# Where the sums of an attention are spread, how 16 leftover keys are multiplied, and how a final norm ends: three edits in one fused decoder kernel

## The chip, the core and the metric

The kernel runs on one core of a Trainium2 chip. The time is the device time of one execution in microseconds (us); lower is better. The engines are TensorE (PE in the profile, its weight loads PEld), VectorE (DVE), ScalarE (ACT), GpSimd (POOL) and SyncE (SP), which here issues nearly all transfers.

## What is computed

The reference is two layers of a decoder with two groups of heads. 16 learned "meta" tokens stand ahead of 512 tokens (T = 528), the model width D is 1024, all in float32. Per layer:

```python
xn = rmsnorm(h, attn_norm_g)
proj = xn @ w_in                      # q,k,v of 8 FoX heads (64 wide), a gate each; q,k,v,g of 4 retention heads (128 wide)
logf = log_sigmoid(flog + b_fgate)
# FoX: softmax(q.k / 8 + c[t] - c[s]) v over s <= t, with c = cumsum(logf)
# retention: sum over s <= t of gamma^(t-s) (q.k) v, then a group norm per head, times silu(g)
h = h + concat(fox, ret) @ w_out
hn = rmsnorm(h, ffn_norm_g)
h = h + (silu(hn @ w_gate) * (hn @ w_up)) @ w_down      # 2816 wide
```

Meta queries form a block of their own, real queries go in blocks of 128. After the second layer comes `rmsnorm(h, final_norm)`, and the first 16 tokens are dropped.

## The kernel before

**Layout and products.** Activations lie transposed: 128 features on the partitions, the 528 tokens along the free dimension. Each float32 operand is split into a high part that TensorE's fast float32 format holds exactly, and a low part (`split`, L136 to L138: ScalarE casts to `hi`, VectorE subtracts to get `lo`), so a product is two or three matmuls (`hi*hi`, `hi*lo`, `lo*hi`). Weights come from DRAM through SP into three `raw` buffers (L153); ScalarE casts them (L186), and GpSimd or VectorE subtract (L187). An output tile of a projection needs 24 matmuls of 264 columns twice (L210).

**Order.** TensorE's list is written out by hand: `layer` builds a `plan` in which the steps of attention and retention are merged at given places into the 128-wide projections (`merge`, `spread`, `ret_places`), and `manual_schedule` holds TensorE to it. The instructions of VectorE, ScalarE, GpSimd and SP are put in order by the scheduler, each engine works through its list in order, and `tc.high_priority()` moves what stands in it forward. PSUM has 8 banks: 4 in a ring `psa` (`psum_a()`) for scores, transposes and attention products, the rest for projections (`psd`). Scratch tiles of 128x528 in SBUF, called by tags as `tt("tq")`, `tt("ol")`, `tt("sq")`, `tt("sd")`, come from one ring "w" of four.

**FoX heads** go in four pairs per layer (`fox_steps`). `values` (transposes at L409) turns the pair's values into five blocks of keys: four of 128, and the last one of 16. `scores(s, b)` makes the scores of head s and query block b (L497), the bias and row minimum (L503, L504, L509) and the exponential on ScalarE with the row sums accumulated (L517). `turn` transposes the probabilities on TensorE (L409) and splits them into `pth` and `ptl`; the last 16 keys of four blocks are turned together by VectorE's 32x32 transpose (L521). `product(s)` multiplies values by probabilities, high and low: with 16 keys in the last block, too, there are two matmuls (L567); in layer 0 the meta queries have two of 16 columns (L559). Then `ol` and `mixt` (L570, L571) put the two halves together. The division by the row sums comes after the second head: at the last `scores` VectorE takes the reciprocal of `sums` (L525), ScalarE spreads it to a [128, 512] tile `tq` (L527), and in `product(1)` four transposes (L576) turn this into a PSUM bank, by which VectorE multiplies (L577). The result is split into `mxh`, `mxl` for the output projection.

**Retention heads** (`ret_steps`): `values` transposes (L409), subtracts the mean (L662, L663) and splits into `rvh`, `rvl`. `scores` multiplies q by k (L694), then VectorE by the decay (`sd`, L699), then a split into `rsh`, `rsl`; the last 16 keys go to small tiles `rs`. `product` (L724) has three matmuls per key block, so also for the last 16 keys.

**The end.** In the last layer the down-projection is in two column ranges, PA (272 columns) and PB (240). While the rows m = 0 to 7 of range b are made, `after_0` to `after_7` carry the norm of range a between them: squares, sums over rows by a matmul with ones (L1135), the reciprocal root as `Ln` and then `Exp` on ScalarE (L1122, L1123), one Newton step of three VectorE rows (L1127, L1129, L1131), and multiplications by the root (L1110), each followed by a store (L1113). GpSimd does out_a 0 and 2 and out_b 6; VectorE does the others. For range b everything after row 7 is behind the last matmul of the down-projection.

## Time and profile before

| | |
|---|---|
| runs | 1278.76, 1278.95, 1279.9 us; median 1278.95 |
| profiled execution | 1278.89 us, its span 1277.1 us |
| granted TensorE clock | 0.996 |
| instructions | 23190, of them 9265 matmuls |

The span is what the profile covers, from the first to the last instruction on the core; the execution's time is 1.8 us longer. Busy time is the time in which an engine had an instruction at work. Rows of the timeline give the start in us, the duration in us, the engine, the line, the operation, output and input, and the shape; where several rows of one kind follow closely they are joined, and xN says how many. In square brackets stands the idle time before a row, and what ended it.

### The profile page before, as it was taken

How to read it: one execution, taken by the hardware profiler on the slowest of the kernel's cores; microseconds unless marked ns; L12 is line 12 of the kernel's file. 1: busy time of each engine (PE TensorE's matmuls, PEld its weight loads, DVE VectorE, ACT ScalarE, POOL GpSimd, SP SyncE). 2: the span in 40 equal slices, each digit the busy share in tenths (PEclk: the TensorE clock that was granted, in tenths of full speed). 3: DMA queues.
4: the chain of work that ended last, by engine and by line, in shares of the span. 5: the costliest groups of instructions: out<-in, count | busy, mean ns of one | idle time of the engine just before them, and what ended most of it. 6: DMA issues, size and time to landing. Idle time of an engine off the chain costs nothing.

```text
span 1277.1 us, 23190 instructions
## 1 busy us (share of the span) xinstructions
PE 1258.0 (99%) x9265; PEld 1197.8 (94%) x9265; DVE 1019.4 (80%) x1849; ACT 687.7 (54%) x1250; POOL 181.0 (14%) x150
## 2 busy tenths in 40 slices
PE   9999999999999999999999999999999999999997
PEld 8899999999999999999999989999789999999996
DVE  7888866879988888887687878568899878888867
ACT  7566655576544444444455665456764444444445
POOL 2233333210000000000014334332000000000001
PEclk9999999999999999999999999999999999999998
DMA  6222222223323333332323122222223333333321
GB/s 233 76 67 84 75 84 84 66 73 115 107 97 100 100 100 100 100 100 83 100 76 112 65 100 84 77 91 66 100 83 130 102 100 100 100 100 100 103 79 67
DMA packets 45677, 120.55 MB, mean 94 GB/s; under 512 B 5360, under 2 KB 12272, under 8 KB 45568
## 3 DMA queue, kind: packets, MB, share of 16 engines
q1 hardware_dynamic: 45136, 118.77, 28.4%
q8 instruction: 73, 1.20, 0.4%
q10 hardware_dynamic: 432, 0.29, 0.1%
q14 instruction: 36, 0.29, 0.1%
HBM read 116.91 MB, written 2.13 MB: 93 GB/s over the span
## 4 chain that ended last, share of the span: by engine, by line
PE 84%; DVE 10%; ACT 4%; DMA 1%; issue 1%; DVEq 0%; POOL 0%; ACTq 0%
PE psd L210 24%; PE psa L875 18%; PE psd L1010 14%; PE psd L875 13%; PE psa L1010 4%; PE psa L210 3%; PE psa L409 2%; PE psa L497 1%; PE psa L567 1%; PE psa L724 1%; PE psa L694 1%; DVE qs L429 1%; DMA bc<-cdr 1%; DVE pr L504 1%; DVE rsl L138 0%
## 5 line engine op out<-in xcount | busy, mean ns | idle before, releaser
L187 POOL TENSOR_TENSOR wlo<-raw,whi 128x512 fp32r<-128x512 f32 x126 | 172.3, 1381 | 380.2 <-ACT whi L186 380.2
L210 PE MATMUL psd<-xh,whi 128*128 128x264 f32 (+1 forms) x792 | 195.8, 315 | 0.0
L210 PE MATMUL psd<-xl,whi 128*128 128x264 f32 (+1 forms) x792 | 186.5, 303 | 0.6 <-DVE xl L313 0.6
L210 PE MATMUL psd<-xh,wlo 128*128 128x264 f32 (+1 forms) x792 | 186.9, 303 | 0.0
L210 PEld LDWEIGHTS psd<-xh,whi 128*128 128x128 f32 x792 | 128.7, 190 | 4.7 <-ACT whi L186 0.4
L210 PEld LDWEIGHTS psd<-xh,wlo 128*128 128x128 f32 x792 | 127.2, 188 | 6.2 <-DVE wlo L187 0.4
L210 PEld LDWEIGHTS psd<-xl,whi 128*128 128x128 f32 x792 | 128.0, 189 | 5.2 <-DVE xl L313 1.2
L186 ACT CAST whi<-raw 128x512 fp32r<-128x512 f32 (+1 forms) x168 | 98.3, 613 | 39.2 <-PE psd L210 19.9
L863 ACT CAST whi<-raw 128x1024 fp32r<-128x1024 f32 (+2 forms) x62 | 54.9, 885 | 51.3 <-PE psd L875 39.9
L863 ACT CAST fwhi<-raw 128x1024 fp32r<-128x1024 f32 (+2 forms) x62 | 55.6, 897 | 48.1 <-PE psd L875 40.5
L864 DVE TENSOR_TENSOR wlo<-raw,whi 128x1024 fp32r<-128x1024 f32 (+2 forms) x62 | 62.9, 1014 | 13.7 <-ACT whi L863 13.6
L864 DVE TENSOR_TENSOR fwlo<-raw,fwhi 128x1024 fp32r<-128x1024 f32 (+2 forms) x62 | 64.0, 1032 | 10.8 <-ACT fwhi L863 10.5
L875 PE MATMUL psa<-th,whi 128*128 128x264 f32 (+1 forms) x232 | 65.4, 282 | 0.0
L875 PE MATMUL psa<-th,wlo 128*128 128x264 f32 (+1 forms) x232 | 65.4, 282 | 0.0
L875 PE MATMUL psa<-tl,whi 128*128 128x264 f32 (+1 forms) x232 | 65.3, 282 | 0.0
L875 PE MATMUL psa<-th,fwhi 128*128 128x264 f32 (+1 forms) x224 | 63.4, 283 | 0.0
L875 PE MATMUL psa<-tl,fwhi 128*128 128x264 f32 (+1 forms) x224 | 63.3, 283 | 0.0
L875 PE MATMUL psa<-th,fwlo 128*128 128x264 f32 (+1 forms) x224 | 63.3, 282 | 0.0
L517 ACT ACTIVATE pr<-pr,nmax 128x144 f32<-128x144 f32 (+1 forms) x64 | 36.9, 576 | 42.8 <-DVE nmax L504 30.5
L941 ACT COPY e<-psa 128x264 f32<-128x264 f32 (+1 forms) x114 | 42.9, 376 | 27.9 <-PE psa L875 23.6
L863 ACT CAST fwhi<-S 128x1024 fp32r<-128x1024 f32 x20 | 21.0, 1049 | 68.6 <-PE psa L875 66.5
L1010 PE MATMUL psd<-ah,fwlo 128*128 128x264 f32 (+1 forms) x200 | 56.6, 330 | 0.0
(355 smaller groups left out, 4008.6 us busy)
## 6 DMA issues: line engine op xcount, KB each, us to landing
raw<-w_in SPq DMA_DIRECT2D x54, 512.0 KB, 3.5
raw<-w_gate SPq DMA_DIRECT2D x44, 512.0 KB, 4.0
fraw<-w_up SPq DMA_DIRECT2D x38, 512.0 KB, 3.4
raw<-w_down SPq DMA_DIRECT2D x64, 256.0 KB, 2.7
raw<-w_out SPq DMA_DIRECT2D x16, 512.0 KB, 3.5
raw<-w_down SPq DMA_DIRECT2D x32, 192.0 KB, 2.5
bc<-cdr SPq DMA_DIRECT2D x16, 264.0 KB, 3.3
raw<-w_up SPq DMA_DIRECT2D x6, 512.0 KB, 3.5
```

The costliest lines, as they stand in the source:

```text
L186: pin(nc.scalar.copy(hi, job["raw"][:, c0:c1]), pinned)
L187: pin(sub(lo, job["raw"][:, c0:c1], hi.bitcast(F32)), pinned)
L210: nc.tensor.matmul(ps[1][b][:, 0:c1 - c0], w[:, wk, :], x[:, c0:c1], start=(k == 0 and i == 0), stop=(k == n - 1 and i == 2))
L409: nc.tensor.transpose(ps[:, 128 * j:128 * j + 128], src[:, o:o + 128], idt)
L429: nc.vector.tensor_sub(sv(t, real, b0, b1), sv(tq, real, a0, a1), sv(t, real, a0, a1).bitcast(F32))
L497: nc.tensor.matmul(sc[0:nq, 0:c1 - c0], st["q"][s][:, q0:q0 + nq], kk[:, c0:c1], start=(i == 0), stop=(i == 1))
L517: nc.scalar.activation(pr, pr, AF.Exp, bias=nmax[0:nq], scale=-1.0, accum_out=rsum)
L863: nc.scalar.copy(hi, src)
L864: nc.vector.tensor_sub(lo, src, hi.bitcast(F32))
L875: nc.tensor.matmul(bank()[:, 0:b.shape[-1]], a[:, o + k, :], b, start=(fresh and k == 0 and i == 0), stop=(k == n - 1 and i == 2), skip_gr ...
L941: nc.scalar.copy(self.t["e"][:, i], self.t["x"][:, 0:w])
L1010: nc.tensor.matmul(v[:, 0:c1 - c0], a[:, s * n + k, :], b[:, c0:c1], start=(k == 0 and i == 0), stop=(k == n - 1 and i == 2))
```

## The change

It has three parts.

**The sums' way (FoX).** The row sums of a pair lie in one of two persistent [128, 32] tiles. At the last `scores` step VectorE takes the reciprocals and turns the tile in 32x32 squares, both with priority. Four SP transfers write the turned rows to a DRAM tile [8, 128], two more read them back, each spread over 64 partitions, into a `tq` tile. `product(1)` multiplies `mixt` by this tile in SBUF. The four transposes, their PSUM bank and ScalarE's spread go.

**The last 16 keys, stacked.** The last block's 16 keys take 16 of 128 partitions. Now partitions 0 to 15 hold the high part, 32 to 47 the low part, and the values stand a second time on the same partitions (`repeat`, a ScalarE copy in `v_done`), so one matmul does both. The meta block of layer 0 lies at partitions 64 and 96 of the same tile with a third and fourth copy of values. In retention, high, low and again high parts (partitions 0, 32, 64) stand against the values' high part twice and low part once, so one matmul takes the place of three.

**The end.** All multiplications by the root are VectorE's, GpSimd has none. The reciprocal root is one ScalarE activation, `Abs_reciprocal_sqrt`, whose table set is loaded after the last silu in place of the one for logarithms. The steps `after_3` to `after_7` are put in another order: all three Newton rows of range a in `after_3`, its multiplications 0 and 2 in `after_3` and `after_4`; the low part of the sum of squares is made in `after_6`, and the last sums go in the order high, low, square 6, square 7 behind square 5.

```diff
+    sum_tiles = [state.tile([128, 32], F32, name=f"sums{i}") for i in range(2)]
+    for t in sum_tiles:
+        nc.gpsimd.memset(t, 0.0)
...
+    def repeat(vt, c0, n, at):
+        nc.scalar.copy(vt[:, at:at + 32 * n].rearrange("p (n c) -> p n c", c=32)[:, :, 0:META],
+                       vt[:, c0:c0 + META].unsqueeze(1).broadcast_to([128, n, META]))
...
@@ FoX v_done
+            repeat(vt, SEQ, 1, SEQ + 32)
+            if not real:
+                repeat(vt, 0, 2, SEQ + 64)
...
@@ FoX scores, last step
-                nc.vector.reciprocal(st["sums"], st["sums"])
-                st["rows"] = tt("tq")
-                nc.scalar.copy(st["rows"][:, 0:SEQ].rearrange("p (b s d) -> p b s d", b=NBLK, s=2),
-                               st["sums"].unsqueeze(3).broadcast_to([128, NBLK, 2, 64]))
+                sums = sum_tiles[g % 2]
+                turned = tmp.tile([128, 32], F32, name="turned", tag="turned")
+                with tc.high_priority():
+                    nc.vector.reciprocal(sums[:, 0:2 * NBLK], sums[:, 0:2 * NBLK])
+                    nc.vector.transpose(turned, sums)
+                rdr = tc.dram_tile([2 * NBLK, 128], F32, name=f"rdr{ly['l']}{g}")
+                for a in range(4):
+                    nc.sync.dma_start(rdr[:, 32 * a:32 * a + 32], turned[32 * a:32 * a + 2 * NBLK, :])
+                st["rows"] = tt("tq")[:, 0:SEQ]
+                wide = rdr.rearrange("(s b) q -> s (b q)", s=2)
+                for i, (a0, a1) in enumerate(ROWS):
+                    nc.sync.dma_start(st["rows"][a0:a1], wide[i:i + 1, :].partition_broadcast(64))
...
@@ FoX turn
-                split(pth[0:META, 0, 0:META], ptl[0:META, 0, 0:META], e[0:META, 0:META])
+                nc.scalar.copy(pth[64:64 + META, 4, 0:META], e[0:META, 0:META])
+                nc.vector.tensor_sub(pth[96:96 + META, 4, 0:META], e[0:META, 0:META], pth[64:64 + META, 4, 0:META].bitcast(F32))
...
-                split(*[corners(t)[0:META, 1:] for t in (pth, ptl)], st["ends"][0:META, :, 32 - META:32])
+                e = st["ends"][0:META, :, 32 - META:32]
+                nc.scalar.copy(corners(pth)[0:META, 1:], e)
+                nc.vector.tensor_sub(corners(ptl)[0:META, 1:4], e[:, 0:3], corners(pth)[0:META, 1:4].bitcast(F32))
+                nc.vector.tensor_sub(pth[32:32 + META, 4, SEQ:T], e[:, 3], pth[0:META, 4, SEQ:T].bitcast(F32))
...
@@ FoX product
-                for i, pp in enumerate(pt):
-                    nc.tensor.matmul(po[:, 0:META], v[:, 0, :], pp[:, 0, 0:META], start=(i == 0), stop=(i == 1))
+                nc.tensor.matmul(po[:, 0:META], v[:, 4, :], pt[0][:, 4, 0:META], start=True, stop=True)
...
-                for i, pp in enumerate(pt):
+                for i, pp in enumerate(pt if j < 4 else pt[:1]):
...
-                rb = psum_a()
-                for b in range(NBLK):
-                    nc.tensor.transpose(rb[:, 128 * b:128 * b + 128], st["rows"][:, 128 * b:128 * b + 128], idt)
-                nc.vector.tensor_mul(mt[:, META:T], rb, mt[:, META:T])
+                nc.vector.tensor_mul(mt[:, META:T], st["rows"], mt[:, META:T])
...
@@ retention v_done, values, scores, product
+            repeat(vr, SEQ, 2, SEQ + 32)
...
-                split(vh[:, j0:j0 + n], vl[:, j0:j0 + n], c)
+                if j0 < 4:
+                    split(vh[:, j0:j0 + n], vl[:, j0:j0 + n], c)
+                else:
+                    nc.scalar.copy(vh[0:64, 4], c[0:64, 0])
+                    nc.scalar.copy(vl[64:128, 4], c[64:128, 0])
+                    nc.vector.tensor_sub(vh[64:128, 4], c[64:128, 0], vl[64:128, 4].bitcast(F32))
...
-                split(eh[0:kn], el[0:kn], sd[0:kn, full:used])
+                d4 = sd[0:kn, full:used]
+                nc.scalar.copy(e[0:kn], d4)
+                nc.vector.tensor_sub(e[32:32 + kn], d4, e[0:kn].bitcast(F32))
+                nc.scalar.copy(e[64:64 + kn], d4)
...
-                for i, (a, b) in enumerate(((vh, sh), (vh, sl), (vl, sh))):
...
+                    nc.tensor.matmul(po[:, SEQ - META:SEQ], vh[:, 4, :], kept["e"], start=False, stop=True)
...
@@ the end
             def root(r, v):
-                pin(nc.scalar.activation(r, v, AF.Ln, bias=epsc, scale=1.0 / D))
-                pin(nc.scalar.activation(r, r, AF.Exp, scale=-0.5))
+                pin(nc.scalar.activation(r, v, AF.Abs_reciprocal_sqrt, bias=epsc, scale=1.0 / D))
...
             def after_3():
-                a = fin["ra"], fin["va"], fin["ta"]
+                for i in range(3):
+                    newton(i, fin["ra"], fin["va"], fin["ta"])
                 sum_b(2)
-                newton(0, *a)
-                newton(1, *a)
                 square_b(3)
-                scale_b(0, 1)
+                out_a(0)
+                scale_b(0)
...
             def after_4():
-                newton(2, fin["ra"], fin["va"], fin["ta"])
...
-                out_a(nc.gpsimd, 0)
-                out_a(nc.gpsimd, 2)
+                out_a(2)
+                scale_b(1)
...
             def after_7():
...
-                sums(v, (fin["one"][0], hi, fin["one"][1], lo, fin["one"][2]))
+                sums(v, (fin["one"][0], hi, lo, fin["one"][1], fin["one"][2]))
+                out_a(4)
+                out_a(6)
+                scale_b(3)
                 root(fin["rb"], v)
-                out_a(nc.vector, 4)
-                out_a(nc.vector, 6)
-                scale_b(5, 6, 7)
+                scale_b(4, 5, 6, 7)
                 for i in range(3):
                     newton(i, fin["rb"], v, fin["tb"])
-                out_b(nc.gpsimd, 6)
-                for k in (0, 2, 4):
-                    out_b(nc.vector, k)
+                for k in range(0, NK, 2):
+                    out_b(k)
```

More of the change, by code (lines that the diff above doesn't have):

```diff
@@ L97, in enter_att @@
             zero(l, t)
-        end_tiles[:] = [[phase["att"].tile([128, META], F32R, name=f"rs{i}{k}") for k in range(2)] for i in range(2)]
-        for t in end_tiles[0] + end_tiles[1]:
+        end_tiles[:] = [phase["att"].tile([128, META], F32R, name=f"re{i}") for i in range(2)]
+        for t in end_tiles:
             zero(l, t.bitcast(F32))
@@ L395, in forget_sums, with silu @@
         nc.sync.dma_start(st["cdr"], z2)
-    def silu(t, last=False):
+    LOGS = "natural_log_exp_and_others"
+    ROOTS = "abs_reciprocal_sqrt_and_small"
+    def silu(t, then=None):
         nc.scalar.activation(t, t, AF.Silu)
-        if last:
-            tc.keep_in_program_order(nc.scalar.preload_act_table_set("natural_log_exp_and_others"))
+        if then:
+            tc.keep_in_program_order(nc.scalar.preload_act_table_set(then))
     def transpose_into(src, offs):
@@ L512, in scores @@
             else:
-                if (s, b) == (0, 0):
-                    st["sums"] = tmp.tile([128, NBLK, 2], F32, name="sums", tag="sums")
-                rsum = st["sums"][:, b, s:s + 1]
+                rsum = sum_tiles[g % 2][:, NBLK * s + b:NBLK * s + b + 1]
             pr = pt[0:nq, 0:nk]
@@ L721, in product @@
                 if j == 4:
-                    (sh, sl), used = kept["e"], 0
-                for i, (a, b) in enumerate(((vh, sh), (vh, sl), (vl, sh))):
-                    nc.tensor.matmul(po[:, qa - META:SEQ], a[:, j, :], b[:, used + qa - q0:used + T - q0],
-                                     start=(j == 0 and i == 0), stop=(j == 4 and i == 2))
+                    nc.tensor.matmul(po[:, SEQ - META:SEQ], vh[:, 4, :], kept["e"], start=False, stop=True)
+                else:
+                    for i, (a, b) in enumerate(((vh, sh), (vh, sl), (vl, sh))):
+                        nc.tensor.matmul(po[:, qa - META:SEQ], a[:, j, :], b[:, used + qa - q0:used + T - q0],
+                                         start=(j == 0 and i == 0), stop=False)
                 if j == 0 and not real:
@@ L953, in done @@
                 nc.vector.scalar_tensor_tensor(sg[:, c], sg[:, c], RSC, st["R"][:, c], ALU.mult, ALU.mult)
-                silu(sg[:, c], self.f == NF - 1)
+                silu(sg[:, c], None if self.f < NF - 1 else ROOTS if last else LOGS)
                 u = tt("tq")
@@ L1228, in layer @@
         QC = REAL if real else FULL
-        ly, ff = {"wait": []}, {}
+        ly, ff = {"wait": [], "l": l}, {}
         fox = [{} for _ in range(FP)]
```

35 lines of the change are left out of this document (17 added, 18 removed).

## The prediction, made before the changed kernel had run

> **What bounds the kernel now.** I read the page first for the span and the shares, then the view of TensorE's waits, then the timeline of the stages that the diff touches. The page:
>
> ```profile
> span 1277.1 us, 23190 instructions
> PE 1258.0 (99%) x9265; PEld 1197.8 (94%) x9265; DVE 1019.4 (80%) x1849; ACT 687.7 (54%) x1250; POOL 181.0 (14%) x150
> PEclk9999999999999999999999999999999999999998
> PE 84%; DVE 10%; ACT 4%; DMA 1%; issue 1%; DVEq 0%; POOL 0%; ACTq 0%
> ```
>
> TensorE is busy 99% of the span at a clock that is granted throughout, and it carries 84% of the chain that ended last. So a matmul taken out of its list is time gained, as long as no new wait takes its place; work added to the other engines is free only while they keep ahead. How much waiting is left there now, the view of TensorE's waits says (line waited at, releaser, us in total, times, longest); its first three rows of twelve, and the last:
>
> ```profile
> PE psa L567 <- DVE ptl L138: 1.7, 1, 1.7
> PE psa L1256 <- DVE wide L61: 1.6, 1, 1.6
> PE psa L409 <- DVE psa L503: 1.1, 1, 1.1
> ...
> PE psa L497 <- DVE mixt L571: 0.2, 1, 0.2
> ```
>
> The twelve sum to 9.6 us, and all but one end on VectorE. The execution of this profile took 1278.89 us, so 1.8 us lie outside its span; the median of the three runs is 1278.95, which is the same time. Everything below is set against 1278.89. A measurement of this kernel can tell about 0.2%, 2.6 us, from no change.
>
> **Part 1, TensorE's list: 72 of 9265 matmuls go.** Nothing else in its order moves. From the timelines of layer 0's last pair and first retention head:
>
> ```profile
> 258.58 0.26 PE L559 MATMUL psa<-ptl,vv 128*128 128x16 f32 x1
> 258.69 0.47 PE L567 MATMUL psa<-pth,vv 128*128 128x512 f32 x1
> 260.03 0.22 PE L567 MATMUL psa<-pth,vv 128*128 128x16 f32 x1
> 260.10 0.26 PE L567 MATMUL psa<-ptl,vv 128*128 128x16 f32 x1
> 260.21 0.66 PE L576 MATMUL psa<-idt,tq 128*128 128x128 f32 x4
> 260.63 0.49 PE L210 MATMUL psd<-xh,whi 128*128 128x264 f32 x2
> 80.44 0.33 PE L724 MATMUL psa<-rs,rvh 128*128 128x16 f32 x2
> 80.74 0.49 PE L210 MATMUL psd<-xh,whi 128*128 128x264 f32 x2
> ```
>
> Matmuls overlap, so the price of one is the step from its start to the next start, not its duration. A 16-column `ptl` matmul: 258.69-258.58 = 0.11, and 260.21-260.10 = 0.11. There are 16 of them in the large products and 8 in layer 0's meta products: 24 x 0.11 = 2.6. The one that stays loses its 0.07 step (260.10-260.03) and takes a last one's 0.11, at 16 places 0.6 back. Retention's three (two by `rvh`, then one by `rvl`), from 80.44 to the next matmul at 80.74, take 0.30; one stays at 0.11, so 0.19 at each of 8 heads: 1.5. The four transposes of L576 start at 260.21 and the next matmul at 260.63: 0.42 x 8 pairs = 3.4. Together 2.6 - 0.6 + 1.5 + 3.4: **-6.9**. Bounds: 5.9 (the 24 at steps of 0.07) and 7.5 (nothing back).
>
> **Part 2, the sums' way.** Before: reciprocal, ScalarE's spread into a `tq` tile, four transposes, multiplication from a PSUM bank. Now: reciprocal, VectorE's 32x32 turn, four small writes to DRAM, two broadcast reads into the `tq` tile, multiplication from SBUF. The pair with the least time between its two ends is layer 0's third:
>
> ```profile
> 182.06 0.20 DVE L525 RECIPROCAL sums<-sums 128x8 f32<-128x8 f32 x1
> 184.90 6.27 SPq L153 DMA_DIRECT2D raw<-w_in  x2
> 193.15 0.69 DVE L577 TENSOR_TENSOR mixt<-psa,mixt 128x512 f32<-128x512 f32 x1
> 181.73 0.30 DVE L521 STREAM_TRANSPOSE pe<-pr 32x128 f32<-32x128 f32 x1
> 180.33 0.33 SPq L487 DMA_DIRECT2D bc<-cdr  x1
> bc<-cdr SPq DMA_DIRECT2D x16, 264.0 KB, 3.3
> SPq L487 <- DMA cdr<-z: 3.8, 2, 2.7
> L525 DVE RECIPROCAL sums<-sums x8: 203/204/205, 67.4 to 873.3; 128x8 f32<-128x8 f32 x8
> L577 DVE TENSOR_TENSOR mixt<-psa,mixt x8: 691/692/692, 81.0 to 890.0; 128x512 f32<-128x512 f32 x8
> L186 ACT CAST whi<-raw 128x512 fp32r<-128x512 f32 (+1 forms) x168 | 98.3, 613 | 39.2 <-PE psd L210 19.9
> ```
>
> Step by step: 182.06 + 0.20 + 0.30 (a turn, by L521) = 182.6; four writes at 0.33 of issue on SP, to 183.9; their landing is not in the trace, the nearest row is SP's wait for `cdr<-z`, at most 2.7, so 186.6; then the two reads, priced as the `bc` broadcasts from DRAM (3.3 to landing, and those are twice as wide): 190.3. The multiplication comes at 193.15, so **2.8 us to spare**. Between writes and reads the built order puts one weight load on SP, which at this place is issued at 184.90, inside the writes' landing, so it delays nothing. Where this pair has 11.1 us between the two ends, the first pair has 81.0 - 67.4 = 13.6 and the last 890.0 - 873.3 = 16.7, so I cost the transfers at nothing; the cover is the second head's product. Queued behind the waiting reads on SP are the next weight loads, later by up to the 2.7 of the wait; who waits for them is the cast of L186, and half of the idle time before it (19.9 of 39.2) is ended by TensorE giving a buffer back, not by a landing, so they have room. [...] ScalarE gives back eight spreads. The reads hold a `tq` tile of ring "w" until the multiplication, where ScalarE's copy held it to the transposes, a few us less; the ring has four.
>
> [...]
>
> The multiplication now has two operands in SBUF instead of one in PSUM. What GpSimd does to such a row is seen at the end of the kernel:
>
> ```profile
> 1264.12 2.84 POOL L1110 TENSOR_TENSOR th<-th,e 128x544 f32<-128x544 f32 x2 [360.62 <-ACT sq L1103]
> 1264.51 1.25 DVE L1106 TENSOR_TENSOR S<-S,sq 128x240 f32<-128x240 f32 x1
> 1263.87 0.40 DVE L1106 TENSOR_TENSOR S<-S,sq 128x240 f32<-128x240 f32 x1
> ```
>
> The same addition takes 0.40 alone and 1.25 under GpSimd's multiplication, ending as that one ends. So each of the eight new multiplications can lose up to 1.3 us to a `wlo` subtraction (1381 ns mean in the groups). [...] The multiplication gates only the mix cast, and the output projection comes later, so I cost it at 0 and keep 0 to 2.6 (two pairs hit on the path).
>
> **Part 3, what the new order makes late.** ScalarE gets 36 small copies (repeated values and keys, third copies of ends) for 8 long ones, and the reciprocal goes ahead with priority; so VectorE and ScalarE do some things in another order. The cost is where TensorE comes right behind. From the timelines:
>
> ```profile
> 70.32 0.71 DVE L138 TENSOR_TENSOR rsl<-sd,rsh 128x528 fp32r<-128x528 f32 x1 [0.73 <-ACT rsh L137]
> 71.24 0.40 PE L724 MATMUL psa<-rsl,rvh 128*128 128x512 f32 x1
> 71.98 0.48 ACT L137 CAST pth<-psa 128x384 fp32r<-128x384 f32 x1
> 251.23 1.20 DVE L699 TENSOR_TENSOR sd<-psa,dec 128x264 f32<-128x264 f32 x3
> 253.50 0.71 PE L409 MATMUL psa<-idt,pd 128*128 128x128 f32 x5
> 254.88 0.87 DVE L662 TENSOR_REDUCE mean<-psa 128x4 f32<-128x512 f32 x2
> ```
>
> (a) Layer 0, third retention head: the built order puts `mean` (the wide one of the two, about 0.5 of the 0.87) ahead of two `sd` multiplications, which stood before it at 251.23. The fifth `pd` transpose needs the bank that these free, so TensorE waits for 0.5 + two of the three in 1.20 (0.8), about 1.2, and 0.3 for a `ptl` pushed behind. (b) Layer 0, first head: the 128x384 `pth` cast (0.48) and its `ptl` move ahead of `rsh`/`rsl`; `rsl` ends at 71.03 and is read at 71.24, so about 1.0 shows. (c) Layer 1's first head has the same with half of it in front: 0.5. (d) Layer 1's last pair, second product, where a `ptl` comes late: 0.6, and 0.2 in small ones. Sum **+3.8**. Bounds: -2 (one PSUM bank fewer per pair, so some of the 9.6 us of today's waits may go; SP's and ScalarE's work moves too) and +9 (about 1.1 at each of eight pairs, the size of the third row of the waits, 1.1).
>
> **Part 4, the end.**
>
> ```profile
> 1268.11 0.46 ACT L1122 ACTIVATE S<-psa,epsc 128x240 f32<-128x240 f32 x1 [0.89 <-PE psa L1135]
> 1268.60 0.40 ACT L1123 ACTIVATE S<-S 128x240 f32<-128x240 f32 x1
> 1270.36 2.23 DVE L1110 TENSOR_TENSOR tl<-tl,S 128x480 f32<-128x480 f32 x2
> 1270.47 1.60 POOL L1110 TENSOR_TENSOR tl<-tl,S 128x480 f32<-128x480 f32 x1 [3.50 <-DVE S L1131]
> 1272.51 0.65 DVE L1110 TENSOR_TENSOR tl<-tl,S 128x480 f32<-128x480 f32 x1
> ```
>
> VectorE loses GpSimd's locks (0.85 at L1106, 1.0 in the last `tl` rows) and takes three multiplications more (0.65 each). The first two come before the sums end, so the last square's addition is later, and the root starts at about 1268.6 instead of 1268.11 (an estimate: 0.65 less what the lost locks leave free there). It is one activation of 0.46, to 1269.1, where two ended at 1269.00. The three newton steps take as long as before, 1270.36 - 1269.00 = 1.36: 1270.45. Rows of VectorE overlap by 0.08 (1272.51 against 1270.36 + 2.23), so four multiplications take 3 x 0.57 + 0.65 = 2.36: 1272.8, where 1272.51 + 0.65 = 1273.16 stood. That is 0.35, and as much again because the four last stores come evenly and not bunched behind GpSimd's: **-0.7**. Bounds: -1.2 (the sums not later) and +0.3 (VectorE a multiplication behind).
>
> **Sum:** -6.9 + 0 + 3.8 - 0.7 = -3.8: 1278.89 - 3.8 = **1275.1**.
>
> **The rivals.** All is hidden: the waits of part 3 vanish because the ring of banks has one user less per pair; -6.9 - 0.7 = -7.6, **1271.3**. For it: only twelve waits today. Against it: (a) and (b) have no slack in the rows. The waits eat it: part 3 at three quarters of its upper bound, +6.8 for 3.8, **1278.1**, not to be told from no change. For it: VectorE is 80% busy, and it ends all but one of the waits. The end does not do what it says: VectorE, alone now, is late with the squares; +0.3 for -0.7, with the waits 0.7 over the forecast, 1276.8. [...]
>
> **How the numbers follow.** Forecast 0.49, all hidden 0.13, waits eat it 0.20, the end 0.07, rows late 0.11. Faster by over 0.2% (below 1276.3) is the first two, 0.62; within 0.2% the third and fourth, 0.27; slower 0.11. The range reaches from 1270.8, the hidden case with part 1 near its upper bound, to 1280.3, the waits at their +9 with the rest as forecast; the slow rival lies outside.
>
> **What would show it.** In the changed profile: 9193 matmuls; no L576 transposes; TensorE busy about 7 us less; the multiplication by the rows without idle VectorE time ahead of it on a DMA; new rows in TensorE's waits at the `pd` transposes and at `rsl`, some 4 us over today's 9.6; one root of 0.46 and last stores 0.7 earlier behind the last down-projection matmul. A wait for a DMA at the multiplication, or a sum of TensorE's waits over 17 us, would make the prediction wrong.

## The result and the profile after

The changed kernel takes **1281.89 us** (median of 16 runs, 1280.49 to 1285.47) beside 1278.83 for the kernel before in the same rounds (16 runs, 1277.28 to 1279.9). The measured ratio is 1.0029, 95% interval [1.0022, 1.0036]; it is the measurement's own and not exactly the quotient of the medians. So the change costs about 3 us where I had forecast a gain of 3.8, and the time lies outside my range. The profiled execution took 1280.8 us, 1.8 more than its span.

The page of the kernel after:

```profile
span 1279.0 us, 23180 instructions
PE 1252.3 (98%) x9193; PEld 1189.7 (93%) x9193; DVE 1028.4 (80%) x1874; ACT 690.9 (54%) x1276; POOL 176.9 (14%) x148
PE 80%; DVE 13%; ACT 5%; issue 1%; DMA 1%; DVEq 0%; ACTq 0%
```

The 72 matmuls are gone and TensorE is busy 5.7 us less, yet the span is 1.9 longer. In the chain that ended last TensorE lost 4% and VectorE gained 3%: the time went into waiting. The view of TensorE's waits of the kernel after, three of its 22 rows (line waited at, releaser, us in total, times, longest):

```profile
PE psa L591 <- DVE ptl L147: 3.9, 2, 2.2
...
PE psa L421 <- DVE sd L725: 1.2, 1, 1.2
...
PE psa L754 <- DVE rsl L147: 1.0, 2, 0.7
```

The rows sum to 18.8 us, where the twelve of before summed to 9.6: **9.2 us of new waits**. One of them, 0.7 at L1162 where 0.2 stood before, lies behind the last down-projection matmul and so belongs to the end; ahead of it 8.7 are new. I had 3.8 for them, and had written that a sum over 17 would prove the prediction wrong.

The listed waits are not the whole price. Pair TensorE's rows of the two profiles in order: the last down-projection matmul starts 2.5 us later than before (1267.86 for 1265.37). On the way to it, 7.7 are gained where matmuls went. Another 1.6 are gained because the profile of before ran 3.4 us at a granted clock of 0.50 and this one ran at 1.00 there (more on that below). Against these stand 10.1 lost at the places where the idle time changed, and 1.7 in steps too small to be listed. The view counts idle time from the end of the matmul before, but without a wait the next matmul starts 0.1 to 0.2 ahead of that end (886.42 behind a matmul from 886.11 to 886.58, below); so a listed wait makes TensorE later than it says.

The largest new wait is in layer 1's last pair, ahead of the second product. TensorE's timeline, before and then after:

```profile
886.11 0.47 PE L567 MATMUL psa<-pth,vv 128*128 128x512 f32 x1
886.42 0.40 PE L567 MATMUL psa<-ptl,vv 128*128 128x512 f32 x1
...
887.46 0.21 PE L567 MATMUL psa<-pth,vv 128*128 128x16 f32 x1
...
888.05 0.48 PE L210 MATMUL psd<-xh,whi 128*128 128x512 f32 x1
```

```profile
886.90 0.48 PE L591 MATMUL psa<-pth,vv 128*128 128x512 f32 x1
889.07 0.50 PE L591 MATMUL psa<-ptl,vv 128*128 128x512 f32 x1 [1.68 <-DVE ptl L147]
...
890.21 0.22 PE L591 MATMUL psa<-pth,vv 128*128 128x16 f32 x1
890.28 0.47 PE L219 MATMUL psd<-xh,whi 128*128 128x512 f32 x1
```

The end of this product shows the gain: from the last key block's matmul to the projection it was 0.59 and is 0.07, so 0.52 of matmul time is saved. Its beginning shows the loss: the step from `pth` to `ptl` was 0.31 and is 2.17, so 1.86 is lost. Of these 1.86 the view of waits lists 1.68. The loss is made some ten us earlier, on ScalarE. Its timeline before, from behind the last exponential and the `rkh` cast, and two rows of VectorE:

```profile
873.62 0.62 ACT L527 COPY tq<-sums 128x512 f32<-128x512 f32 x1
874.14 0.68 ACT L288 ACTIVATE r<-psa,epsc 128x512 f32<-128x512 f32 x1
874.86 0.63 ACT L289 ACTIVATE r<-r 128x512 f32<-128x512 f32 x1
875.56 0.62 ACT L137 CAST rsh<-sd 128x512 fp32r<-128x512 f32 x1
876.15 0.24 ACT L137 CAST pth<-pe 16x64 fp32r<-16x64 f32 x1
```

```profile
874.84 0.69 DVE L699 TENSOR_TENSOR sd<-psa,dec 128x512 f32<-128x512 f32 x1 [0.59 <-PE psa L694]
...
885.59 0.68 DVE L138 TENSOR_TENSOR ptl<-psa,pth 128x512 fp32r<-128x512 f32 x1
```

And ScalarE after, with VectorE's rows of the same stretch in a second fence:

```profile
876.97 0.25 ACT L572 CAST pth<-pe 16x64 fp32r<-16x64 f32 x1 [2.77 <-PE psa L591]
877.91 0.27 ACT L146 CAST pth<-psa 128x128 fp32r<-128x128 f32 x1 [0.69 <-PE psa L421]
878.07 0.69 ACT L297 ACTIVATE r<-psa,epsc 128x512 f32<-128x512 f32 x1
...
879.27 0.63 ACT L298 ACTIVATE r<-r 128x512 f32<-128x512 f32 x1
```

```profile
877.25 0.20 DVE L573 TENSOR_TENSOR ptl<-pe,pth 16x48 fp32r<-16x48 f32 x1 [2.18 <-ACT pth L572]
...
877.68 0.69 DVE L725 TENSOR_TENSOR sd<-psa,dec 128x512 f32<-128x512 f32 x1
...
888.32 0.69 DVE L147 TENSOR_TENSOR ptl<-psa,pth 128x512 fp32r<-128x512 f32 x1
```

This is the new thing to see. ScalarE's spread (L527) is gone, and what fills its place is the cast of the last 16 keys (L572). That cast writes `pth`, which TensorE still reads for the first head's product, so it stands at the head of ScalarE's queue for 2.77 us; the two root activations that ran at 874.14 and 874.86 run at 878.07 and 879.27. VectorE waits for the same cast (2.18), with the first `sd` behind it, which before started at 874.84 and now at 877.68. Both engines then have the same work with some 2.5 us less, and the last `ptl` of the pair comes at 888.32 where it came at 885.59.

The transfers, for whose lateness I had kept a chance of 0.11 ("rows late"), are in time. SP's and VectorE's rows in layer 0's third pair, then the multiplication by the rows over all eight pairs (lines of one operation: times in all, shortest, median and longest in ns, first and last start):

```profile
183.37 1.30 SPq L545 DMA_DIRECT2D rdr<-turned  x4
186.29 1.09 SPq L549 DMA_DIRECT2D tq<-rdr  x2
194.06 0.69 DVE L597 TENSOR_TENSOR mixt<-tq,mixt 128x512 f32<-128x512 f32 x1
```

```profile
L597 DVE TENSOR_TENSOR mixt<-tq,mixt x8: 691/692/939, 80.8 to 891.9; 128x512 f32<-128x512 f32 x8
```

From the last write's issue (184.67) to the first read's (186.29) it is 1.6, so the reads were issued 0.3 ahead of the 186.6 that I had. That it came so close is partly luck: the issue of the writes ended 0.8 later than the 183.9 of the sum, and the wait behind them was 1.6 in place of the 2.7 allowed. The multiplication comes 6.7 after the second read's issue, and does not wait for it; the reads (`tq<-rdr`) land 2.8 to 3.7 after their issue, median 3.2. One multiplication of eight takes 0.94 and the others 0.69. The long one starts at 718.92, while a `wlo` subtraction of GpSimd runs until 719.32; the other seven meet no work of GpSimd. So of the bound of 2.6 that I had kept for two pairs hit by GpSimd 0.25 came.

Layer 0's fourth retention head (my "third": I had counted one short) has the wait that I foresaw, on TensorE and VectorE:

```profile
254.12 0.66 PE L421 MATMUL psa<-idt,pd 128*128 128x128 f32 x4 [0.29 <-DVE ptl L147]
255.99 0.30 PE L421 MATMUL psa<-idt,pd 128*128 128x128 f32 x1 [1.21 <-DVE sd L725]
```

```profile
254.81 0.69 DVE L683 TENSOR_REDUCE mean<-psa 128x4 f32<-128x512 f32 x1 [0.75 <-PE psa L421]
255.42 0.76 DVE L725 TENSOR_TENSOR sd<-psa,dec 128x264 f32<-128x264 f32 x2
```

`mean` waits for four of the transposes, `sd` stands behind it, and the fifth transpose needs the bank that `sd` frees: 0.29 + 1.21 = 1.5 listed, as forecast.

The end after, last down-projection matmul to last stores:

```profile
1267.86 0.28 PE L905 MATMUL psa<-ah,fwlo 128*128 128x240 f32 x1
1271.06 0.46 ACT L1150 ACTIVATE S<-psa,epsc 128x240 f32<-128x240 f32 x1 [0.38 <-PE psa L1162]
1272.89 2.36 DVE L1140 TENSOR_TENSOR tl<-tl,S 128x480 f32<-128x480 f32 x4
1273.61 2.04 SPq L1141 DMA_DIRECT2D out_t<-tl  x4
```

The root is one activation of 0.46 and the four multiplications take 2.36, both as written. From the last matmul's start to the span's end it is 1279.0 - 1267.86 = 11.1; before it was 1277.1 - 1265.37 = 11.7 (that matmul's row before starts at 1265.37), so **-0.6** where I had -0.7.

### The profile page after: what moved, and what is told of

The parts are those of the page before. It is cut to its first block, busy times and chain, and to the rows that moved or that the text cites. A ratio compares the mean times of both kernels' runs of the same rounds, so it can differ in the third digit from the quotient of the medians.

```text
span 1279.0 us, 23180 instructions
## 1 busy us (share of the span) xinstructions
PE 1252.3 (98%) x9193; PEld 1189.7 (93%) x9193; DVE 1028.4 (80%) x1874; ACT 690.9 (54%) x1276; POOL 176.9 (14%) x148
## 4 chain that ended last, share of the span: by engine, by line
PE 80%; DVE 13%; ACT 5%; issue 1%; DMA 1%; DVEq 0%; ACTq 0%
PE psd L219 22%; PE psa L905 18%; PE psd L1040 14%; PE psd L905 13%; PE psa L1040 4%; PE psa L219 3%; PE psa L421 1%; PE psa L512 1%; PE psa L591 1%; DVE pr L519 1%; PE psa L754 1%; PE psa L720 1%; DVE ptl L147 1%; ACT whi L195 1%; DVE qs L441 1%
## 5 line engine op out<-in xcount | busy, mean ns | idle before, releaser
L219 PE MATMUL psd<-xh,wlo 128*128 128x264 f32 (+1 forms) x792 | 186.6, 303 | 0.0
```

Source lines behind the costliest of these rows:

```text
L219: nc.tensor.matmul(ps[1][b][:, 0:c1 - c0], w[:, wk, :], x[:, c0:c1], start=(k == 0 and i == 0), stop=(k == n - 1 and i == 2))
```

## The experiments

The experiments set three theories against one another. **ORDER:** without ScalarE's spread the scheduler puts other work at the heads of ScalarE's and VectorE's queues, and it is these orders that cost the time. **TRANSFERS:** the six small transfers per pair, or SP's waits for them, cost it. **COPIES:** the 36 small copies that stacking gives to ScalarE cost it. The medians stand as kernel / before in the same job.

**The parts, each alone in the kernel before.** The first four runs take one part each from the diff of the change, whole; of each its central line:

```diff
e1, the sums' way:
-                    nc.tensor.transpose(rb[:, 128 * b:128 * b + 128], st["rows"][:, 128 * b:128 * b + 128], idt)
+                nc.vector.tensor_mul(mt[:, META:T], st["rows"], mt[:, META:T])
e2, the FoX keys stacked:
-                for i, pp in enumerate(pt):
+                for i, pp in enumerate(pt if j < 4 else pt[:1]):
e3, the retention keys stacked:
+                    nc.tensor.matmul(po[:, SEQ - META:SEQ], vh[:, 4, :], kept["e"], start=False, stop=True)
e4, the end:
+                pin(nc.scalar.activation(r, v, AF.Abs_reciprocal_sqrt, bias=epsc, scale=1.0 / D))
```

> The kernel before with the sums' way alone (32 transposes, 8 spreads on ScalarE and a PSUM bank per pair less; 48 small transfers more). Worked out gain on TensorE 3.4 us. Theory ORDER (the loss of the changed kernel is the new order that the scheduler gives VectorE and ScalarE, above all the cast of the 16x64 key ends, which without the spread in front of it reaches the head of ScalarE's queue while TensorE still reads the tile that it overwrites): waits at the fourth pair of layer 1 as in the changed kernel (about 2 us), some elsewhere, in sum 2 to 5, so between -1.4 and +1.6 against before. Rival TRANSFERS (the small transfers delay the weight loads and the multiplication): carries the whole loss, +3 or more, and the waits end on weight casts. Rival COPIES (the small ScalarE copies of the stacking are the loss): -3.4, with no new wait.

> The kernel before with only FoX's last 16 keys stacked (24 matmuls less, 12 small ScalarE copies more). Gain on TensorE 2.0 us. COPIES: waits of 3 us or more at the transposes of the values, so +1 or more against before. ORDER: the spread on ScalarE is still there, so no 2 us wait at the fourth pair of layer 1; other places up to 2, so -2 to 0. TRANSFERS: -2.0.

> The kernel before with only retention's last 16 keys stacked (16 matmuls less, 24 small ScalarE copies more, the fifth value block turned after them). Gain on TensorE 1.5 us. COPIES: waits of 2 us or more at the retention heads, +0.5 or more. ORDER: the mean ahead of the decay multiplications at layer 0's third head would show here if the stacking makes it (about 1.4 there), so about 0; without it -1.5. TRANSFERS: -1.5.

> The kernel before with only the new end (no GpSimd, one reciprocal root). Everything up to the last down-projection stays, so all theories say the same: about -0.5, from the comparison of the two traces behind the last matmul of the down-projection (2.32 us late there, the span 1.9 late), and within what can be told from no change; +0.3 or more if VectorE, alone with all multiplications, is the end's bound.

| | median / before | ratio [95%] | TensorE's waits, us |
|---|---|---|---|
| e1, sums' way | 1283.33 / 1279.12 | 1.0042 [1.0030, 1.0055] | 14.8 |
| e2, FoX stacked | 1278.71 / 1279.12 | 0.9996 [0.9988, 1.0005] | 12.3 |
| e3, retention stacked | 1279.33 / 1279.12 | 1.0002 [0.9993, 1.0012] | 11.2 |
| e4, the end | 1277.71 / 1279.12 | 0.9989 [0.9980, 0.9997] | 10.0 |

The sums' way costs by itself more than the whole change, though it takes 32 matmuls away. The +4.2 lies above the -1.4 to +1.6 that ORDER had given it, and in the range of TRANSFERS; but its new waits end on VectorE, not on weight casts as TRANSFERS has it. The end gains 1.4 in medians, and 1.0 behind the last down-projection matmul of its profile (10.8 for 11.7); 0.7 was forecast. The stackings give nothing that can be told from none. The four differences of medians add up to +2.6, and the whole has +3.1. The waits of e1 have the two largest new rows of the change, at the same places:

```profile
PE psa L576 <- DVE ptl L141: 3.8, 2, 2.0
...
PE psa L412 <- DVE sd L704: 1.1, 1, 1.1
```

e2 and e3 show why the stackings give nothing: their waits are 2.7 and 1.6 over the 9.6 of before, against 2.6 - 0.6 = 2.0 and 1.5 of matmuls saved by my count. Paired row by row with before, the matmuls that go save 2.6 and 1.8, and the waits take 2.6 and 1.9 back.

**ORDER against TRANSFERS.** e5 gives the changed kernel a useless instruction: ScalarE's old spread, into the tile that the transfers overwrite afterwards. e6 gives the kernel before six useless transfers per pair, the reads a quarter as wide and into a tile that nobody reads; the order of TensorE, VectorE and ScalarE stays.

```diff
e5, on the changed kernel:
+                st["rows"] = tt("tq")[:, 0:SEQ]
+                nc.scalar.copy(st["rows"].rearrange("p (b s d) -> p b s d", b=NBLK, s=2),
+                               sums[:, 0:2 * NBLK].rearrange("p (s b) -> p b s", s=2).unsqueeze(3).broadcast_to([128, NBLK, 2, 64]))
e6, on the kernel before:
+                    nc.sync.dma_start(rdr[:, 32 * a:32 * a + 32], st["rows"][32 * a:32 * a + 2 * NBLK, 0:32])
...
+                    nc.sync.dma_start(spare[a0:a1], wide[i:i + 1, 0:128].partition_broadcast(64))
```

> The changed kernel with ScalarE's spread put back: a 0.62 us copy per pair into the tile that the transfers then overwrite, so it computes nothing that is used. More work and nothing less. In the built order VectorE's decay multiplications stand ahead of the mean again and ScalarE's root rows ahead of the key ends, as before the change. ORDER: the waits at layer 0's fourth retention head (1.4) and at layer 1's fourth pair (2 and more) go, so 3 to 5 us faster than the changed kernel, at or below the kernel before: 1276.5 to 1278.5. TRANSFERS and COPIES: as the changed kernel or slower, 1281.5 to 1283.

> The kernel before with the six transfers per pair added (four writes to DRAM, two broadcast reads, a quarter as wide as in the change, into a tile that nothing reads). The order of VectorE's, ScalarE's and TensorE's instructions is that of the kernel before, to the last row. ORDER: same as before, within 0.3 us. TRANSFERS: slower by 2 us or more, with TensorE or casts waiting for weight loads.

e5 takes 1276.72 / 1278.14, ratio 0.9988 [0.9979, 0.9997]. These eight more copies of 0.62 us make the changed kernel about 4.5 us faster (-1.4 against before where it had +3.1), and faster than the kernel before. e6 takes 1278.64 / 1278.14, 1.0001 [0.9992, 1.0009], with 9.7 us of waits: the transfers cost nothing. e5 carries them at their full width, and its reciprocal and turn have the same priority as in the changed kernel, so neither of these is the cause. ScalarE's timeline of e5 in layer 1's last pair:

```profile
871.70 0.61 ACT L544 COPY tq<-sums 128x512 f32<-128x512 f32 x1
872.22 0.68 ACT L297 ACTIVATE r<-psa,epsc 128x512 f32<-128x512 f32 x1
...
873.99 0.62 ACT L146 CAST rsh<-sd 128x512 fp32r<-128x512 f32 x1 [0.43 <-DVE sd L727]
```

Behind the useless copy the roots and `rsh` come in the order of before, and nobody stands idle for 2 us; the last pair's wait and the one at `sd` are gone from the list, whose sum is 14.2 for 18.8. Paired row by row with e5, the changed kernel's TensorE falls back by more than 0.15 at five sites only: 1.0 at layer 0's first retention head, 1.8 at its fourth, 0.5 at layer 1's first, 0.6 at a transpose at 762.00 and 1.6 in the last pair, 5.5 together. ORDER holds; TRANSFERS is out.

**Holding single rows back.** If the order is the cause, three rows put where they stood should do as well as the spread. (The cast of the last 16 keys is also written with the turn of the first block, where it was written with that of the last.)

```diff
e9, on the changed kernel:
+                if (s, b) == (1, 0):
+                    tc.keep_in_program_order(cast)
...
-            if b == blocks[-1]:
...
+            if b == 0:
...
+                tc.keep_in_program_order(nc.scalar.copy(corners(pth)[0:META, 1:], e))
...
+                    if (l, hd, j0) == (0, 3, 0):
+                        tc.add_manual_dep(mean_sum.ins, last["sd"].ins.name, mybir.DependencyInfo(
+                            mybir.DependencyClass.NoSync, mybir.DependencyReason.DATA), reason="order")
```

> The changed kernel with three rows held back on their engines, nothing else: the first cast of the second head's probabilities and the cast of the key ends stay behind what ScalarE had before them in the program, and at layer 0's fourth retention head the mean stays behind the decay multiplications. ORDER: the wait of 1.4 at that head goes and the one of about 2 at layer 1's fourth pair shrinks, other places may change by some tenths: 2 to 3 us faster than the changed kernel, 1278.5 to 1280. TRANSFERS: no gain, 1281.5 or more.

This is a miss: 1284.98 / 1278.14, 1.0052 [1.0039, 1.0064], where 1278.5 to 1280 was expected. Among TensorE's waits of e9:

```profile
PE psa L421 <- DVE sd L732: 2.0, 1, 2.0
PE psa L727 <- DVE ptl L573: 1.8, 2, 1.2
```

The two waits that were aimed at are replaced by two new ones: a row that is held for all eight pairs moves others. In layer 1's last pair, where the 2.0 is, `ol` now stands between the two roots with 2.2 us of waiting; the 1.2 is in layer 0, at 132.87 us, where there was no fault. So the loss again goes with where rows stand, but a hand on single rows does not make it good.

**Everything but the sums' way.** e10 takes the lines of e2, e3 and e4 together.

> The change without the sums' way: both stackings and the new end. Gain on TensorE 3.5 us, end 0.5 to 0.9. The three alone gave medians of -0.4, +0.2 and -1.4 against before, sum -1.6. ORDER: their small ScalarE copies move the order less than the spread does: 1276.5 to 1278. TRANSFERS: -4, 1275. COPIES: slower than before.

e10 takes 1279.0 / 1278.14, 1.0005 [0.9996, 1.0014]; a miss on the slow side. Its waits sum to 13.6, 4.0 over before: the 40 matmuls fewer come back as waits in many places. So COPIES has a part of its own: the stackings do not slow the kernel, but they pay nothing. The next two runs show that this is so with the sums' way, too: e11 below, without the stackings, has -1.5 against before in medians, and e5, with them, -1.4.

**The sums' way with the useless copy.** e12 is e1, and e11 is e1 with e4's end, each with e5's copy.

> The sums' way and the new end, without the stackings, and with ScalarE's unused spread kept. Gain on TensorE 3.4 us, end 0.5 to 0.9. ORDER: the order of VectorE and ScalarE is nearly that of the kernel before, so few new waits: 3 to 4 us faster than before, the best of all so far, 1274 to 1275.5 where before takes 1278.1 to 1279.1. If the stackings were worth their matmuls after all, it is slower than the changed kernel with the spread (which was 1.4 faster than before).

> The sums' way alone with ScalarE's unused spread kept; without the spread it was 4.2 us slower than before. ORDER: the waits of the version without the spread go, the 3.4 us of the transposes are left: 2 to 3.4 faster than before, some 7 us between two kernels that differ by eight copies nobody reads. TRANSFERS: as without the spread, 4 slower than before.

e12 takes 1277.22 / 1277.81, 0.9988 [0.9979, 0.9997], against 1.0042 without the copy. Against before in the same rounds e12 has -0.6 where e1 had +4.2, so one 0.62 us copy per pair is worth about 5 us here. e11 takes 1276.26 / 1277.81, 0.9982 [0.9973, 0.9991]. Both gain less than was expected of them, 2 to 3.4 us for e12 and 1274 to 1275.5 for e11. The eleven runs of e11 fall in two groups, 1274.83 to 1275.34 and 1276.26 to 1277.75, and only the first lies where it was expected. That led to the next question.

**The wait that is left, and the clock behind it.** All kernels so far have a wait of about 2 us at layer 0's first product, before too (the 1.7 at L567, which the prediction shows). The windows view of the kernel before, behind that wait (window, its us, then busy us and count of PE, PEld, DVE, ACT, POOL, the granted clock, DMA share, GB/s), and one window of the kernel after at the same place:

```profile
61.00:62.00 1.00, 1.00 (x7) 1.00 (x6) 0.68 (x1) 0.17 (x1) 0.00 (x0) 0.50 0.00 0
...
63.00:64.00 1.00, 1.00 (x6) 1.00 (x6) 0.32 (x2) 0.00 (x0) 0.00 (x0) 0.50 0.00 0
```

```profile
62.00:63.00 1.00, 1.00 (x10) 1.00 (x10) 0.96 (x5) 0.03 (x1) 0.00 (x0) 1.00 0.00 0
```

In the profiled execution of before the granted clock was 0.50 for 3.4 us after the wait (the five windows from 60 to 65 have 0.98, three times 0.50, and 0.82), with 6 or 7 matmuls in a us instead of 10 or 11. That costs about 1.6 us: over this stretch the kernel after goes from 0.35 behind to 1.31 ahead in the paired rows. In its profile the clock stayed at 1.00, though its wait was longer (2.2). To take the wait away, the step with the first product of layer 0's first pair is moved three projection steps later; TensorE's work stays the same.

```diff
+    def later_from(placed, by):
+        p0, p1 = next(p for p, f in placed if f in later), placed[-1][0]
+        return [(p if p < p0 or not by else p0 + by + (p - p0) * (p1 + 2 - p0 - by) / (p1 - p0), f) for p, f in placed]
...
-                          spread(main, *m0), spread(rest, *r0), ret_places(g, *places))
+                          later_from(spread(main, *m0), 3.0 if l + g == 0 else 0), spread(rest, *r0), ret_places(g, *places))
```

e15 is e11 with this, e16 the kernel before with it, e17 the changed kernel with it. e13 and e14 are first attempts on e11, 2.5 and 3.5 steps by another rule, which puts the first head's product behind rows of the second head in the same tile: there 16 meta columns of one head are made with the second head's probabilities, in e14 the first block of 128 queries too (its cast comes at 59.01, the product at 60.34). So these two do not compute what the reference does, and only their times are used.

> The fastest so far (sums' way, new end, unused spread kept), with one thing moved in TensorE's list: in layer 0's first pair the first head's product comes behind two more projection steps and the next scores, some 1.9 us of matmuls, where TensorE stands for 1.8 us today for the low part of the probabilities. In the runs so far the granted clock is 0.50 for some 3 us behind that wait in one execution and 1.00 in another of the same kernel, and the times of a kernel fall in two groups about 1.5 us apart with mean clocks of 0.998 and 0.996. Theory DIP (the lower clock follows the wait): no execution under 0.998 is left, one group of times, and 1.7 faster than the fast group: about 1273.3, median 1273 to 1274. Rival (the lower clock comes whatever TensorE did): 1.7 faster in both groups, the two groups stay, median 1274.5.

> As the run before with the product one projection step later still, behind the next head's first transpose. DIP: as there, within 0.5 us. If the wait only moves to another matmul, the two groups come back.

> The fastest version (sums' way, new end, unused spread kept) with the first head's product of layer 0's first pair three projection steps (18 matmuls, 2.2 us) later in TensorE's list, and what follows it there in its order behind it, so that it computes what the reference does. Theory DIP: the wait of 1.8 us goes and with it the lower clock: one group of times, all at a mean clock of 0.998 or more, 1273.5 to 1274.5. Rival: the lower clock comes whatever TensorE did: two groups about 1.5 apart.

> The kernel before with the same step later and nothing of the change: the price of that wait in the kernel before. DIP: its two groups (1277.2 to 1277.9 at 0.998, 1278.4 to 1279.6 at 0.996 to 0.997) become one, at 1276 to 1277. So the change's own balance is seen without the lower clock. Rival: two groups, both 1 lower.

> The changed kernel with the same step later. Of its two waits of some 2 us the first goes, the second (layer 1's fourth pair) stays. DIP: still two groups, because of the second wait, about 1.7 below those of the changed kernel: 1279 and 1280.5. Rival (only the first wait's place brings the lower clock): one group, near 1279.

| | median (lowest to highest) | ratio to before [95%] |
|---|---|---|
| e13 | 1274.29 (1274.13 to 1274.45) | 0.9971 [0.9959, 0.9982] |
| e14 | 1274.49 (1274.09 to 1275.84) | 0.9973 [0.9963, 0.9984] |
| e15 | 1274.03 (1273.45 to 1274.57) | 0.9964 [0.9952, 0.9977] |
| e16 | 1277.15 (1276.51 to 1278.70) | 0.9992 [0.9983, 1.0001] |
| e17 | 1282.89 (1281.99 to 1285.94) | 1.0038 [1.0026, 1.0051] |

All have 1278.36 for the kernel before. **e15 beats both kernels**, by 4.3 us in medians the one before. It came as expected, in one group, and so nearly did e13 (median 1274.29 for 1273 to 1274) and e16 (1277.15 for 1276 to 1277, one run apart from the group). TensorE's timeline of e15 at the moved product, and the first and longest row of its waits:

```profile
59.55 0.48 PE L585 MATMUL psa<-pth,vv 128*128 128x512 f32 x1
59.87 0.39 PE L585 MATMUL psa<-ptl,vv 128*128 128x512 f32 x1
```

```profile
PE psa L1265 <- DVE wide L61: 1.6, 1, 1.6
```

No wait for a `ptl` is listed any more, the sum is 10.1, and the runs lie within 1.1 us of one another. e15 against e16, with the same moved step, is the sums' way and the end at their worth: 3.1 us in medians; 32 matmuls by my steps (8 x 0.42 = 3.4) and 0.6 at the end would make 4.0. e17 is a miss: 1.7 of gain were expected, but the wait moved on to the next product, and the last pair's stays:

```profile
PE psa L758 <- ACT rsh L146: 1.8, 1, 1.8
PE psa L595 <- DVE ptl L147: 1.7, 1, 1.7
```

There, too, a stretch at 0.50 follows the first of the two (72 to 75 us in its profile). In the changed order, moving one step of TensorE's list does not help.

## Why the prediction was wrong

**Part 1, the matmuls: right.** Places and prices hold. A tail of a product went from 0.59 to 0.07, and retention's three 16-key matmuls from 0.30 to one at 0.07 (79.51 to 79.58 in the profile after; its step was taken as 0.11). The "0.6 back" that I had charged did not come. In the paired rows the saving is 7.7, at its upper bound of 7.5 rather than at 6.9.

**Part 2, the transfers: right, and shown.** e6 has them at 1.0001 [0.9992, 1.0009]. The case "rows late" did not happen: the reads land within 3.7 of their issue, and the kernel is slower by another way. (The 190.3 for the reads holds one more issue of 0.33 that the text does not name; 186.6 + 0.33 + 3.3 is 190.2.) In part 2 stands also the sentence that turned out to matter, "ScalarE gives back eight spreads": I took it as relief, and e1, e5 and e12 show the missing spread as the change's dearest item.

**Part 3, the new waits: this step failed.** It forecast +3.8; the view of waits has +8.7 ahead of the last down-projection matmul, and by the paired rows 10.1 are lost at waits and 1.7 in small steps. Its sites (a), (b) and (c) are there with about their sizes: 1.5 listed for 1.5 (though the text's 0.5 + 0.8 is 1.3, not 1.2); 1.0 for 1.0 by the starts, of which the rows list 0.36 and 0.25 as idle; 0.7 for 0.5. The rows of (b), after:

```profile
70.23 0.49 PE L754 MATMUL psa<-rsh,rvh 128*128 128x512 f32 x1 [0.36 <-ACT rsh L146]
70.98 0.50 PE L754 MATMUL psa<-rsl,rvh 128*128 128x512 f32 x1 [0.25 <-DVE rsl L147]
```

Site (d), layer 1's last pair, "where a `ptl` comes late", was mis-sized: 0.6 forecast, 1.86 measured. I had priced the late `ptl` by itself, and not the two engines that stand 2 to 3 us behind the cast at the head of ScalarE's queue. And "0.2 in small ones" is the larger error. The listed waits of (a) to (d) are 1.5 + 0.6 + 0.7 + 1.7, and layer 0's first product has 0.45 more, together 4.95. Of the 8.7 that leaves about 3.7, in waits that are new or longer by 0.2 to 0.5 at a dozen places. So about the upper bound that I had worked out, +9, is what came in the list, and more than that by the starts. I gave it a fifth of the chance by way of the rival "the waits eat it", whose mechanism was the right one and whose price, 6.8, was still too low.

**Part 4, the end: right,** -0.6 for -0.7 in the profile, and -1.0 in that of e4; e4 alone has 0.9989 [0.9980, 0.9997]. What the sum calls GpSimd's locks no run shows as such; the rows show longer times beside GpSimd's multiplications. An addition of the squares took 1.25 there before (L1106), and the four of after, where GpSimd has none of these multiplications, 0.40 each (L1136); VectorE's three `tl` rows of before took 0.65, 0.66 and 1.65 (L1110), with GpSimd's of 1.60 beside them, and the four of after 2.36 together.

**What no step had:** the clock. I had read the row of nines as a clock "granted throughout". But a digit stands for 32 us, and 9 for 90% or more, so 3.4 us at half the clock do not show in it; the mean of 0.996 was the only sign. The profiled execution of before, against which I made the sum, contains such a stretch, worth some 1.6 us, and that of after contains none. Set like for like the change costs more than the spans show, 1.9 + 1.6 = 3.5.

What stays open: why the scheduler puts the cast of the last 16 keys first once the spread is gone (ScalarE's rows show that it does, and e5 that the spread undoes it), and whether the small waits of the stackings could be placed away; e9 shows only that three rows held by hand do not do it.

## What to carry to other kernels

An instruction on an engine that is 54% busy can still be worth more than it costs, by what it keeps from the head of the queue (e5: eight copies of 0.62 us, and the kernel some 4.5 us faster): before work is taken off a scheduled engine, read which instruction will stand there next, what that one waits for, and what stands behind it. With TensorE 98% busy, matmuls that were saved in small pieces came back here as small waits: the two stackings saved 3.5 us of matmuls by my count and gained nothing (e2 0.9996, e3 1.0002). Whether they stay saved when VectorE and ScalarE also get ahead was not tried. And a forecast that prices only the sites that can be named should add the bound for those that can't.

## What the runs showed of the hardware

- **Behind a wait of TensorE of about 2 us the granted clock was 0.50 in some profiles and 1.00 in others.** Before: 1.75 us idle up to 59.10, then 0.50 granted from 61 to 64 us. After: 2.2 us idle at the same place, and 1.00 throughout. The seventeen profiles list seventeen waits of TensorE of 1.7 to 2.5 us. The windows views of before, after, e1, e2, e3 and e17 cover nine of them. Behind five (the first product's of before, e2 and e3, e1's second and e17's first) comes a stretch at 0.50, which starts between 0.1 us ahead of the wait's end (e2) and 1.9 us behind it (before), and in each case lasts 3.4 us (e2, by us from 59 to 63: 0.69, 0.50, 0.50, 0.60). Behind the other four (both of after, e1's first, e17's second) it is 1.00. In the profiles of before and after no other stretch under 1.00 comes ahead of TensorE's last matmul, and the wait of 1.6 us at their start has none behind it; the profiles of e13 to e16, whose longest wait is 1.6, have mean clocks of 0.998 or 0.999. The windows view of e1, behind its 2.0 us wait at 888.88, and of e17, behind its 1.8 us wait at 70.70:

```profile
891.00:892.00 1.00, 1.00 (x4) 0.76 (x3) 0.93 (x2) 0.98 (x2) 0.00 (x0) 0.50 0.67 274
```

```profile
73.00:74.00 1.00, 1.00 (x6) 1.00 (x6) 0.00 (x0) 0.00 (x0) 0.00 (x0) 0.50 0.00 0
```

  Each kernel has one profile, so these clocks of 0.50 and 1.00 are those of different kernels, where e13's expectation speaks of one kernel; from run to run of one kernel only the mean clock can be read. By it the runs fall in groups some 1.5 us apart: those of the changed kernel with a mean clock of 0.998 took 1280.49 to 1281.62, those with 0.997 took 1282.16 to 1282.82, those with 0.994 to 0.996 took 1283.08 to 1285.47. Without such a wait the runs of e13 and e15 lie within 0.3 and 1.1 us. Those of e14 and e16 lie within 1.8 and 2.2, but their slowest run has a mean clock of 0.998, so something else made it slow. What decides between two executions was not tried.
- **Six small transfers per pair on SP cost no time** that can be measured: e6 has 1.0001 [0.9992, 1.0009], with reads a quarter as wide as the change's. In the profile after, a pair has four writes to DRAM of 1.0 KB and two reads of 128 KB, and in layer 0's third pair the first read followed 1.6 us behind the last write's issue.
